# Keeping pre-computed weight sums in DRAM as two rounded halves

## The chip, the core and the metric

The kernel runs on one core of a Trainium2 chip. The metric is the device time of one execution in microseconds, as a median of runs. The engines are named as in the profile: PE multiplies matrices (PEld loads its stationary operand), DVE and ACT work on elements, POOL does small work, SP issues the DMAs.

## What is computed

A small decoder of two layers on 1024 tokens of width 1024, in float32. Layer 0 mixes tokens by a causal convolution module, layer 1 by sliding-window attention. Each layer then has a squared-ReLU MLP of width 4096 and a gated embedding, with layer norms between them. The part that matters here:

```python
def sq_relu_mlp(x, w_up, w_down):
    return jnp.square(jax.nn.relu(x @ w_up)) @ w_down
...
        x = layer_norm(DEEPNORM_ALPHA * x + sq_relu_mlp(x, mlp_w_up[i], mlp_w_down[i]),
                       mlp_ln_g[i], mlp_ln_b[i])
        x = x + (p[i] @ ple_w_proj[i]) * jax.nn.sigmoid(x @ ple_w_gate[i])
```

## The kernel before

**Arithmetic.** PE multiplies a rounded form of float32 (F32R). To keep precision each operand is split into a high half (the value rounded) and a low half (the value less its high half), and a product is three matmuls: high by high, high by low, low by high (`mm3`, line 676). Splitting costs one ACT cast and one DVE subtraction. On top of that the large products use a recursive scheme with seven block products in place of eight, which needs sums and differences of blocks of the weights: for the up weights S1 to S4 of a pair of units, for the down and gate weights t1 to t4.

**Weights ahead.** Some of that work is done well before it is needed. `low_half` (575) casts a half unit of 512 columns on ACT, subtracts on DVE in place and stores the low half in DRAM. `pair_ahead` (598) forms the four sums of a pair of up units, stores each sum in the DRAM tile `keep` (form in the trace) and its low half in another. `seven_ahead` (629) does the same for a quarter of the gate weights or half of the last chunk of the down weights: it forms t1 to t4, stores each sum (gate_t and down_t in the trace) and each low half (gate_low_t, down_low_t), and the low halves of three blocks that need no sum (gate_low_b, down_low_b). `pair_ahead` is called for one pair in layer 0 and two in layer 1, in the token-mixing stage (`PAIRS_AHEAD`, 74); `seven_ahead` in the up stage, at six points that `UP_WORK` (71) gives, with buffers from two quiet tiles (tag Q, which the trace shows as xh and xl).

**Weights used.** `prep` (549) brings a unit of 1024 columns into two buffers, wh and wl. Where a low half lies in DRAM it loads the sum into a third buffer, raw, casts raw to wh on ACT, and loads wl from DRAM. `Stream` (482) hands units out in the order of their use and refills a slot when the product that read it is done; there are 5 slots of wh and of wl, and 2 of raw (`SLOTS`, 48). In the last chunk of the down stage (`down_seven`, 1481, with `end`) a quarter t1 to t4 is loaded whole into a wl buffer by `quarter` (1476), and `form` (1450) casts it to the operand in two halves and loads the low half. The operands rotate over eight places in the xh and xl tiles, two for each product.

**The order of the work.** The program is first recorded and then ordered by a planner (`schedule`, 328). It goes through the recorded operations with a cost for each, assigns buffers first come, first served, and writes out one order for each engine; SP's DMA issues are among them. `later`, `after` and `slack` only shift priorities. Every instruction is issued from one place, so all have the same line, L479, in the trace; they are told apart by their tiles. Each engine executes its own list in order: an instruction that waits holds back what stands behind it.

**The gate stage** (`ple`, 1608) multiplies a 1024 by 1024 weight by seven block products in the order b11, b21, t4, t3, t2, t1, b22, two units each, four token tiles each.

Of the kernel before, what the change touches and what calls it, by code (L numbers as in the profile page):

```python
# [10 lines left out]
F32 = mybir.dt.float32  # L11
F32R = mybir.dt.float32r
AF = mybir.ActivationFunctionType
ALU = mybir.AluOpType

P = 128
T = 1024
# [3 lines left out]
HT = 512  # L21
# [490 lines left out]
class Emit:  # L512
# [33 lines left out]
        return self.nc.tile(tag, (P, HT), F32, "PSUM")  # L546


    def prep(self, ap, blocks=None, low=None):

        nc = self.nc
        raw = nc.tile("raw", (P, 1024), F32)
        wh = nc.tile("wh", (P, 1024), F32R)
        wl = nc.tile("wl", (P, 1024), F32R)
        if blocks:
            for j, kb in enumerate(blocks):
                cs = slice(j * 256, (j + 1) * 256)
                x = self.sb("X")
                for w, k in ((x, 0), (raw[:, cs], 1))[:: -1 if kb else 1]:
                    nc.sync.dma_start(w, ap[:, cs] if k else self.d["xT"][kb, :, 0:HT])  # L560
                self.split(raw[:, cs], wh[:, cs], wl[:, cs])
                self.split(x, *self.xs(kb, 0, HT))
            return wh, wl
        if low is not None:
            c = slice(0, low.n)
            nc.sync.dma_start(raw[:, c], ap)
            nc.scalar.copy(wh[:, c], raw[:, c])
            nc.sync.dma_start(wl.bitcast(F32)[:, c], low)
            return wh, wl
        nc.sync.dma_start(raw, ap)  # L570
        nc.scalar.copy(wh, raw)
        nc.vector.tensor_tensor(out=wl, in0=raw, in1=wh.bitcast(F32), op=ALU.subtract)
        return wh, wl

    def low_half(self, low, k, tag, raw):
# [4 lines left out]
        nc.vector.tensor_tensor(out=h, in0=raw, in1=h.bitcast(F32), op=ALU.subtract)  # L580
        nc.sync.dma_start(low[:, k * HT : (k + 1) * HT], h.bitcast(F32))

    def dram(self, name, n):
        self.nc.slots(name, [name])
        return self.nc.tile(name, (P, n), F32, "DRAM")
# [12 lines left out]
    def pair_ahead(self, i, f, tag):  # L598

        nc = self.nc  # L600
        w0, w1 = (self.d["w_up"][i, f + k] for k in range(2))
        keep = self.dram(f"form{i}_{f}", 4 * HT)
        low = [self.dram(f"form{i}_{f}_{k}", HT if k == 3 else 2 * HT) for k in range(4)]

        def form(k, out, x, y, op):
            nc.vector.tensor_tensor(out=out, in0=x, in1=y, op=op)
            nc.sync.dma_start(keep[:, k * HT : (k + 1) * HT], out)
            self.low_half(low[1 + k // 2], k % 2, tag, out)

        r1L, r1R, r0L = self.load(tag, w1, 0), self.load(tag, w1, 1), self.load(tag, w0, 0)  # L610
        self.low_half(low[3], 0, tag, r1R)
        form(1, r1R, r1L, r1R, ALU.add)
        form(2, r1L, r0L, r1L, ALU.subtract)
        self.low_half(low[0], 0, tag, r0L)
        form(0, r0L, r1R, r0L, ALU.subtract)
        r0R = self.load(tag, w0, 1)
        self.low_half(low[0], 1, tag, r0R)
        form(3, r0R, r0R, r0L, ALU.subtract)
        aps = w0, keep[:, 0 : 2 * HT], keep[:, 2 * HT : 4 * HT], w1[:, HT : 2 * HT]
        return [lambda ap=ap, l=l: self.prep(ap, low=l) for ap, l in zip(aps, low)]  # L620

    def seven_forms(self, name, n):

# [5 lines left out]
    def seven_ahead(self, name, quarters, k, tag):  # L629

        nc, g = self.nc, self.seven[name]
        b11, b21, b12, b22 = (self.load(tag, ap, c) for ap, c in quarters)

        def low(f, v):
            self.low_half(g[f][1], k, tag, v)

        def form(f, out, x, y):
            nc.vector.tensor_tensor(out=out, in0=x, in1=y, op=ALU.subtract)
            nc.sync.dma_start(g[f][0][:, k * HT : (k + 1) * HT], out)
            low(f, out)  # L640

        for f, v in (("b11", b11), ("b21", b21), ("b22", b22)):
            low(f, v)
        form("t1", b12, b12, b11)
        form("t2", b22, b22, b12)
        form("t3", b11, b22, b11)
        form("t4", b21, b21, b22)

    def work(self, what, k, tag):

# [11 lines left out]
    def gate_units(self, i, n):  # L662

        w, low = self.seven[f"gate{i}"][n]
        r = []
        for m in range(2):
            c = slice(m * 2 * HT, (m + 1) * 2 * HT)
            ap = w[:, c] if w else self.d["w_gate"][i, int(n[2]) - 1, 2 * int(n[1]) - 2 + m]
            r.append(lambda ap=ap, l=low[:, c]: self.prep(ap, low=l))
        return r  # L670

    def split(self, src, h, l):
# [777 lines left out]
    def form(self, src, tag=None, low=None):  # L1450

        hs = slice(0, HT), slice(HT, 2 * HT)
        if tag:
            f = [self.pair(tag, F32R) for k in range(2)]
        else:
            j = self.turn % KB
            self.turn += 1
            q = self.xT[((0, 0), (1, 0), (1, 1), (0, 1))[j // 2]]
            w = [x[:, j % 2 * 2 : j % 2 * 2 + 2, :].rearrange("p a b -> p (a b)") for x in q]
            f = [tuple(x[:, c] for x in w) for c in hs]  # L1460
        if low is not None:
            for k, c in enumerate(hs):
                self.nc.scalar.copy(f[k][0], src[k] if isinstance(src, list) else src[:, c])
                self.nc.sync.dma_start(f[k][1].bitcast(F32), low[:, c])
        elif isinstance(src, list) or tag:
            for k, c in enumerate(hs):
                self.split(src[k] if isinstance(src, list) else src[:, c], *f[k])
        else:
            self.split(src, *w)
        return f  # L1470
# [10 lines left out]
    def down_seven(self, i, cs, start, end, rest):  # L1481
# [6 lines left out]
        nc, d = self.nc, self.d  # L1488
# [3 lines left out]
        own = tags if end else (None, None)  # L1492
# [11 lines left out]
        def A(tag, what):  # L1504
            return load(tag, [self.hid[i][c, what] for c in cs])
# [4 lines left out]
        def halves(tag):  # L1510
            return [list(self.pair(spare)) if start else [self.sb(tag), self.sb(tag)] for c in cs]
# [9 lines left out]
            return out  # L1521

        def product(a, b, to, bank=None, own=(None, None), last=False, low=None, full=()):
            f = [[self.form(v, t, l) for v, t, l in zip(p, own, (None, low and made[low][1]))] for p in zip(a, b)]
            new = bank is None
            bank = [self.ps() for t in range(4)] if new else bank
            if last and to == [(0, 1)]:
                for k in range(3):
                    nc.move("ps", "tr")
            for t in range(4):  # L1530
                for k in range(n):
                    self.part(bank[t], *f[k], t, new and k == 0, k == n - 1, not new)
                for h, q in to:
                    self.add_to(t + 4 * h, q, bank[t], sums if (h, q) in full else None)
            for t in range(4 if last else 0):
                with nc.later(LATE if to == [(0, 1)] else 0):
                    self.layer_norm(t + 4 * to[0][0], gb, None, self.raw, sums[t + 4 * to[0][0]])
            mark = [o for o in nc.ops if o.eng == "tensor"][-1 - 24 * n]
            for k in range(2):
                if rest:  # L1540
                    t = rest.pop(0)
                    self.residual(i, t, tags[t % 2], mark)
            return bank
# [8 lines left out]
        if start:  # L1552
            c = cs[0]
# [5 lines left out]
        else:  # L1559
            a11, b11, a12, b21 = A("wh", (0, 0)), B("wl", 0, 0), None, None  # L1560
        if end:
            made = self.seven[f"down{i}"]
            sm = self.small(2 * NT)
            sums = [sm[:, 2 * t : 2 * t + 2] for t in range(NT)]

            def T(tag, f):
                return [self.quarter(tag, made[f][0])]

            one = product(a11, b11, [(0, 0)], low="b11")
            product(A("raw", (1, 0)), B("wl", 1, 0), [(0, 0)], low="b21", full=[(0, 0)])  # L1570
            product(A("wh", "s2"), T("wl", "t2"), [(1, 0)], one, low="t2")
            product(A("wh", "s1"), T("wl", "t1"), [(1, 1)], one, low="t1")
            s4, b22 = A("wh", "s4"), B("wl", 1, 1)

            self.raw = tuple(nc.tile(f"x{p}01", (P, 4, HT), F32) for p in "lh")
            gb = self.load_row("g", d["mlp_g"][i : i + 1]), self.load_row("g", d["mlp_b"][i : i + 1])
            product(s4, b22, [(0, 1)], one, (None, None), True, "b22", [(0, 1)])
            two = product(A("wh", "s3"), T("wl", "t3"), [(1, 1)], None, own, low="t3", full=[(1, 1)])
            product(A("raw", (1, 1)), T("wl", "t4"), [(1, 0)], two, own, True, "t4", [(1, 0)])
            return  # L1580
        one = product(a11, b11, [(0, 0)], own=("X", "X") if start else (None, None))
        product(a12 or A("raw", (1, 0)), b21 or B("wl", 1, 0), [(0, 0)])
# [511 lines left out]
```

## Time and profile before

| | |
|---|---|
| median of 3 runs | 2132.99 us (2129.67 to 2133.25) |
| profiled execution | 2129.71 us, span 2128.0 us |
| granted TensorE clock | 1.00 |
| busy share PE, PEld, DVE, ACT, POOL | 99%, 82%, 80%, 58%, 13% |
| DMA | 464.00 MB, mean 218 GB/s |

Names in the trace are written out<-in: `wh<-raw` is an instruction that reads raw and writes wh. ps and tr are PSUM banks. Idle time of an engine is given with the instruction that ended it. The stages of layer 0 are the convolution, the mixing of tokens, MLP up (about 445 to 645 us), MLP down (645 to 990), and the gate with the start of attention (990 to 1100); layer 1 has MLP up from 1440, MLP down from 1640 and the gate from 2010 to the end.

### The profile page before, as it was taken

How to read it: one execution, taken by the hardware profiler on the slowest of the kernel's cores; microseconds unless marked ns; L12 is line 12 of the kernel's file. 1: busy time of each engine (PE TensorE's matmuls, PEld its weight loads, DVE VectorE, ACT ScalarE, POOL GpSimd, SP SyncE). 2: the span in 40 equal slices, each digit the busy share in tenths (PEclk: the TensorE clock that was granted, in tenths of full speed). 3: DMA queues.
4: the chain of work that ended last, by engine and by line, in shares of the span. 5: the costliest groups of instructions: out<-in, count | busy, mean ns of one | idle time of the engine just before them, and what ended most of it. 6: DMA issues, size and time to landing. Idle time of an engine off the chain costs nothing.

```text
span 2128.0 us, 29691 instructions
## 1 busy us (share of the span) xinstructions
PE 2111.0 (99%) x9984; PEld 1748.6 (82%) x9984; DVE 1696.3 (80%) x2750; ACT 1239.3 (58%) x2309; POOL 280.1 (13%) x494
## 2 busy tenths in 40 slices
PE   9999999999999999999999999999999999999998
PEld 7888888878888888888787888888888888888877
DVE  8767698978776879876975888699887778888688
ACT  6655654766666533335756889457666663333484
POOL 0000024100000000001421666150000000000042
PEclk9999999999999999999999999999999999999999
DMA  7778954877778747565486022777877785565726
GB/s 255 230 217 281 284 203 155 293 249 268 264 244 258 271 162 227 193 193 183 164 306 224 22 79 83 220 239 255 284 270 261 265 304 176 178 229 171 258 88 219
DMA packets 219609, 464.00 MB, mean 218 GB/s; under 512 B 22080, under 2 KB 55488, under 8 KB 219456
## 3 DMA queue, kind: packets, MB, share of 16 engines
q1 hardware_dynamic: 219456, 462.11, 65.3%
q8 instruction: 78, 1.28, 0.3%
q14 instruction: 75, 0.61, 0.1%
HBM read 314.96 MB, written 147.06 MB: 217 GB/s over the span
## 4 chain that ended last, share of the span: by engine, by line
PE 86%; DVE 4%; ACT 4%; DMA 3%; issue 1%; POOL 1%; SPq 0%; ACTq 0%; POOLq 0%; DVEq 0%
PE ps L479 67%; PE tr L479 18%; ACT z L479 2%; DMA raw<-in_w_up_dram 1%; DVE wl L479 1%; DVE g L479 1%; POOL sm L479 1%; DVE t L479 1%; ACT wh L479 1%; ACT xh L479 1%; ACT t L479 1%; DVE B L479 0%; DMA raw<-in_w_kv_dram 0%; DMA down_low_t<-xl 0%; DVE X L479 0%
## 5 line engine op out<-in xcount | busy, mean ns | idle before, releaser
L479 PE MATMUL ps<-xh,xl 128*128 128x512 f32 x618 | 240.4, 389 | 0.0
L479 PE MATMUL ps<-xl,xh 128*128 128x512 f32 x618 | 240.4, 389 | 0.0
L479 PE MATMUL ps<-xh 128*128 128x512 f32 x618 | 240.4, 389 | 0.0
L479 POOL TENSOR_SCALAR sm<-sm 128x1 f32<-128x1 f32 x72 | 27.0, 379 | 1371.3 <-DVE E L479 610.7
L479 ACT CAST wh<-raw 128x1024 fp32r<-128x1024 f32 (+2 forms) x156 | 142.1, 915 | 105.6 <-PE ps L479 43.5
L479 PE MATMUL ps<-wh,xh 128*128 128x512 f32 (+1 forms) x460 | 182.9, 398 | 2.4 <-DVE t L479 1.5
L479 PE MATMUL ps<-xh,wh 128*128 128x512 f32 x472 | 183.9, 393 | 1.1 <-ACT bo L479 0.4
L479 PE MATMUL ps<-xl,wh 128*128 128x512 f32 x472 | 184.6, 392 | 0.0
L479 PE MATMUL ps<-xh,wl 128*128 128x512 f32 x472 | 184.1, 390 | 0.0
L479 PE MATMUL ps<-wl,xh 128*128 128x512 f32 (+1 forms) x460 | 183.3, 398 | 0.3 <-DMA wl<-gate_low_t 0.3
L479 PE MATMUL ps<-wh,xl 128*128 128x512 f32 (+1 forms) x460 | 182.7, 397 | 0.0
L479 DVE TENSOR_TENSOR wl<-raw,wh 128x1024 fp32r<-128x1024 f32 (+2 forms) x100 | 98.1, 983 | 59.8 <-ACT wh L479 59.4
L479 ACT CAST xh<-wh 128x1024 fp32r<-128x1024 f32 x76 | 79.7, 1049 | 111.8 <-PE ps L479 89.3
L479 ACT CAST wh<-g 128x512 fp32r<-128x512 f32 x136 | 80.9, 620 | 109.0 <-PE ps L479 66.7
L479 PEld LDWEIGHTS ps<-xh 128*128 128x128 f32 x618 | 116.0, 188 | 24.2
L479 PEld LDWEIGHTS ps<-xh,xl 128*128 128x128 f32 x618 | 116.1, 188 | 24.0
L479 PEld LDWEIGHTS ps<-xl,xh 128*128 128x128 f32 x618 | 116.0, 188 | 24.0
L479 DVE TENSOR_TENSOR wl<-g,wh 128x512 fp32r<-128x512 f32 x136 | 89.4, 685 | 35.3 <-ACT wh L479 35.2
L479 ACT ACTIVATE t<-t 128x512 f32<-128x512 f32 x144 | 91.0, 632 | 31.1 <-DVE t L479 29.2
L479 DVE TENSOR_TENSOR xl<-wh,xh 128x1024 fp32r<-128x1024 f32 x76 | 92.7, 1219 | 20.4 <-ACT xh L479 20.4
L479 PEld LDWEIGHTS ps<-xh,wh 128*128 128x128 f32 x472 | 88.8, 188 | 21.1 <-ACT bo L479 0.8
L479 PEld LDWEIGHTS ps<-xh,wl 128*128 128x128 f32 x472 | 88.8, 188 | 18.5
(425 smaller groups left out, 5623.5 us busy)
## 6 DMA issues: line engine op xcount, KB each, us to landing
wh<-hid SPq DMA_DIRECT2D x78, 512.0 KB, 4.2
raw<-in_w_up_dram SPq DMA_DIRECT2D x68, 512.0 KB, 4.2
wl<-in_w_down_dram SPq DMA_DIRECT2D x58, 512.0 KB, 4.8
hid<-zz SPq DMA_DIRECT2D x96, 256.0 KB, 4.7
z<-in_w_dw_dram SPq DMA_DIRECT2D x64, 288.0 KB, 4.3
hid<-t SPq DMA_DIRECT2D x64, 256.0 KB, 4.5
raw<-hid SPq DMA_DIRECT2D x30, 512.0 KB, 3.9
hid<-z SPq DMA_DIRECT2D x36, 256.0 KB, 4.7
```

The source lines that it names most:

```text
L479: getattr(getattr(nc, o.eng), o.name)(*a, **k)
```

## The change

The sums that are made ahead are stored in DRAM as their high half and their low half, and both are loaded as they are. The code that makes them now rounds the sum on ACT, stores the rounded half, subtracts in the place of the sum and stores the rest:

```diff
-    def prep(self, ap, blocks=None, low=None):
+    def prep(self, ap, blocks=None, low=None, halves=False):
 
         nc = self.nc
+        if halves:
+            wh = nc.tile("wh", (P, 1024), F32R)
+            wl = nc.tile("wl", (P, 1024), F32R)
+            for w, src in ((wh, ap), (wl, low)):
+                nc.sync.dma_start(w.bitcast(F32)[:, 0 : low.n], src)
+            return wh, wl
...
+    def high_half(self, high, k, tag, raw):
+
+        nc = self.nc
+        h = self.sb(tag, F32R)
+        nc.scalar.copy(h, raw)
+        nc.sync.dma_start(high[:, k * HT : (k + 1) * HT], h.bitcast(F32))
+        return h
+
+    def rest_half(self, low, k, raw, h):
+
+        nc = self.nc
+        r = raw.bitcast(F32R)
+        nc.vector.tensor_tensor(out=r, in0=raw, in1=h.bitcast(F32), op=ALU.subtract)
+        nc.sync.dma_start(low[:, k * HT : (k + 1) * HT], r.bitcast(F32))
...
-        def form(k, out, x, y, op):
+        def form(out, x, y, op):
             nc.vector.tensor_tensor(out=out, in0=x, in1=y, op=op)
-            nc.sync.dma_start(keep[:, k * HT : (k + 1) * HT], out)
-            self.low_half(low[1 + k // 2], k % 2, tag, out)
+
+        def halves(k, raw):
+            self.rest_half(low[1 + k // 2], k % 2, raw, self.high_half(keep, k, tag, raw))
...
         def form(f, out, x, y):
             nc.vector.tensor_tensor(out=out, in0=x, in1=y, op=ALU.subtract)
-            nc.sync.dma_start(g[f][0][:, k * HT : (k + 1) * HT], out)
-            low(f, out)
+            return f, out, self.high_half(g[f][0], k, tag, out)
...
-        form("t1", b12, b12, b11)
-        form("t2", b22, b22, b12)
-        form("t3", b11, b22, b11)
-        form("t4", b21, b21, b22)
+        t1 = form("t1", b12, b12, b11)
+        t2 = form("t2", b22, b22, b12)
+        rest(*t1)
+        rest(*form("t3", b11, b22, b11))
+        rest(*form("t4", b21, b21, b22))
+        rest(*t2)
...
-        if low is not None:
+        if src is None:
+            for x, ap in enumerate(low):
+                for k, c in enumerate(hs):
+                    self.nc.sync.dma_start(f[k][x].bitcast(F32), ap[:, c])
+        elif low is not None:
...
-            product(A("wh", "s2"), T("wl", "t2"), [(1, 0)], one, low="t2")
+            product(A("wh", "s2"), [None], [(1, 0)], one, low="t2")
```

In `pair_ahead` the order of the steps changes so that a sum is only overwritten after its last use, and `gate_units` and `down_seven` ask for halves where the unit is a sum (t1 to t4). Units without a sum are loaded and cast as before.

More of the change, by code (lines that the diff above doesn't have):

```diff
@@ L603, in pair_ahead @@
         low = [self.dram(f"form{i}_{f}_{k}", HT if k == 3 else 2 * HT) for k in range(4)]
-        def form(k, out, x, y, op):
+        def form(out, x, y, op):
             nc.vector.tensor_tensor(out=out, in0=x, in1=y, op=op)
-            nc.sync.dma_start(keep[:, k * HT : (k + 1) * HT], out)
-            self.low_half(low[1 + k // 2], k % 2, tag, out)
+        def halves(k, raw):
+            self.rest_half(low[1 + k // 2], k % 2, raw, self.high_half(keep, k, tag, raw))
         r1L, r1R, r0L = self.load(tag, w1, 0), self.load(tag, w1, 1), self.load(tag, w0, 0)
         self.low_half(low[3], 0, tag, r1R)
-        form(1, r1R, r1L, r1R, ALU.add)
-        form(2, r1L, r0L, r1L, ALU.subtract)
+        form(r1R, r1L, r1R, ALU.add)
+        form(r1L, r0L, r1L, ALU.subtract)
+        halves(2, r1L)
         self.low_half(low[0], 0, tag, r0L)
-        form(0, r0L, r1R, r0L, ALU.subtract)
+        form(r0L, r1R, r0L, ALU.subtract)
+        halves(1, r1R)
         r0R = self.load(tag, w0, 1)
         self.low_half(low[0], 1, tag, r0R)
-        form(3, r0R, r0R, r0L, ALU.subtract)
+        form(r0R, r0R, r0L, ALU.subtract)
+        halves(0, r0L)
+        halves(3, r0R)
         aps = w0, keep[:, 0 : 2 * HT], keep[:, 2 * HT : 4 * HT], w1[:, HT : 2 * HT]
-        return [lambda ap=ap, l=l: self.prep(ap, low=l) for ap, l in zip(aps, low)]
+        return [lambda ap=ap, l=l, h=j in (1, 2): self.prep(ap, low=l, halves=h) for j, (ap, l) in enumerate(zip(aps, low))]
     def seven_forms(self, name, n):
@@ L638, in form, with rest @@
             nc.vector.tensor_tensor(out=out, in0=x, in1=y, op=ALU.subtract)
-            nc.sync.dma_start(g[f][0][:, k * HT : (k + 1) * HT], out)
-            low(f, out)
+            return f, out, self.high_half(g[f][0], k, tag, out)
+        def rest(f, v, h):
+            self.rest_half(g[f][1], k, v, h)
         for f, v in (("b11", b11), ("b21", b21), ("b22", b22)):
             low(f, v)
-        form("t1", b12, b12, b11)
-        form("t2", b22, b22, b12)
-        form("t3", b11, b22, b11)
-        form("t4", b21, b21, b22)
+        t1 = form("t1", b12, b12, b11)
[4 more added lines that the diff above has]
+        rest(*t2)
     def work(self, what, k, tag):
@@ L668, in gate_units @@
             ap = w[:, c] if w else self.d["w_gate"][i, int(n[2]) - 1, 2 * int(n[1]) - 2 + m]
-            r.append(lambda ap=ap, l=low[:, c]: self.prep(ap, low=l))
+            r.append(lambda ap=ap, l=low[:, c]: self.prep(ap, low=l, halves=w is not None))
         return r
@@ L1523, in product @@
         def product(a, b, to, bank=None, own=(None, None), last=False, low=None, full=()):
-            f = [[self.form(v, t, l) for v, t, l in zip(p, own, (None, low and made[low][1]))] for p in zip(a, b)]
+            f = [[self.form(v, t, l) for v, t, l in zip(p, own, (None, low and (made[low] if p[1] is None else made[low][1])))] for p in zip(a, b)]
             new = bank is None
@@ L1564, in down_seven @@
             sums = [sm[:, 2 * t : 2 * t + 2] for t in range(NT)]
-            def T(tag, f):
-                return [self.quarter(tag, made[f][0])]
             one = product(a11, b11, [(0, 0)], low="b11")
             product(A("raw", (1, 0)), B("wl", 1, 0), [(0, 0)], low="b21", full=[(0, 0)])
-            product(A("wh", "s2"), T("wl", "t2"), [(1, 0)], one, low="t2")
-            product(A("wh", "s1"), T("wl", "t1"), [(1, 1)], one, low="t1")
+            product(A("wh", "s2"), [None], [(1, 0)], one, low="t2")
+            product(A("wh", "s1"), [None], [(1, 1)], one, low="t1")
             s4, b22 = A("wh", "s4"), B("wl", 1, 1)
@@ L1577, in down_seven @@
             product(s4, b22, [(0, 1)], one, (None, None), True, "b22", [(0, 1)])
-            two = product(A("wh", "s3"), T("wl", "t3"), [(1, 1)], None, own, low="t3", full=[(1, 1)])
-            product(A("raw", (1, 1)), T("wl", "t4"), [(1, 0)], two, own, True, "t4", [(1, 0)])
+            two = product(A("wh", "s3"), [None], [(1, 1)], None, own, low="t3", full=[(1, 1)])
+            product(A("raw", (1, 1)), [None], [(1, 0)], two, own, True, "t4", [(1, 0)])
             return
```

## The prediction

> **What bounds the kernel now.** I read the page first: the span and the busy time of each engine.
>
> ```profile
> span 2128.0 us, 29691 instructions
> PE 2111.0 (99%) x9984; PEld 1748.6 (82%) x9984; DVE 1696.3 (80%) x2750; ACT 1239.3 (58%) x2309; POOL 280.1 (13%) x494
> ```
>
> PE, the matmul engine, is idle for 17.0 us of the span (2128.0 - 2111.0). Nothing in the change alters a matmul, so it can only act on those 17 us or add to them. ACT, which it relieves, is busy 58% of the time and is not the bound. The second view is the busy time by stretch, cut at the stages: MLP up (445 to 645), MLP down (645 to 990), the end of layer 0 with its gate (990 to 1100), then the same three of layer 1. The columns are the stretch, its length, then busy time and count of PE, PEld, DVE, ACT, POOL, then clock, DMA share and GB/s.
>
> ```profile
> 445.00:645.00 200.00, 199.41 (x877) 163.87 (x876) 154.95 (x243) 126.39 (x217) 0.00 (x0) 1.00 0.79 264
> 645.00:990.00 345.00, 344.88 (x1522) 285.22 (x1521) 267.04 (x345) 154.07 (x208) 0.00 (x0) 1.00 0.67 223
> 990.00:1070.00 80.00, 78.09 (x372) 63.70 (x372) 71.56 (x125) 59.54 (x108) 33.77 (x39) 1.00 0.35 119
> 1070.00:1100.00 30.00, 28.87 (x148) 23.55 (x147) 25.44 (x34) 20.03 (x34) 7.63 (x6) 1.00 0.92 317
> 1440.00:1640.00 200.00, 199.73 (x879) 164.30 (x878) 166.97 (x264) 133.43 (x228) 0.00 (x0) 1.00 0.81 269
> 1640.00:2010.00 370.00, 370.00 (x1634) 306.43 (x1633) 288.52 (x380) 174.09 (x244) 0.00 (x0) 1.00 0.68 228
> 2010.00:2062.00 52.00, 51.26 (x253) 42.30 (x253) 41.99 (x72) 38.32 (x75) 23.18 (x38) 1.00 0.12 42
> 2062.00:2128.00 66.00, 59.64 (x275) 48.60 (x273) 53.43 (x83) 32.25 (x52) 14.64 (x5) 0.99 0.70 239
> ```
>
> Length minus PE busy is PE's idle time: 0.6 and 0.3 us in the two up stretches, 0.1 and 0.0 in the down stretches, 3.0 from 990 to 1100, 0.7 and 6.4 from 2010 on, most of the 6.4 behind the last matmul. So of the three places where the change works, down offers nothing and the gates offer what there is. The third view, PE's waits, names who ended them (total, times, longest; ps and tr are PSUM banks, released by whoever read them last); the two that a DMA ended are shown where they count.
>
> ```profile
> PE ps L479 <- ACT t L479: 1.1, 3, 0.5
> PE ps L479 <- ACT zz L479: 0.9, 1, 0.9
> PE tr L479 <- ACT zz L479: 0.6, 1, 0.6
> PE ps L479 <- ACT bo L479: 0.4, 1, 0.4
> ```
>
> **Part one: loads and casts.** Three groups of loads change, here with their count, size and median time to landing, and behind them the casts that they feed.
>
> ```profile
> raw<-gate_t SPq DMA_DIRECT2D x16, 512.0 KB, 5.8
> wl<-down_t SPq DMA_DIRECT2D x8, 512.0 KB, 5.1
> raw<-form SPq DMA_DIRECT2D x6, 512.0 KB, 6.1
> L479 ACT CAST wh<-raw 128x1024 fp32r<-128x1024 f32 x111 | 115.9, 1050 | 83.4 <-PE ps L479 31.4 <-DMA raw<-in_w_gate_dram 17.4 <-PE tr L479 16.4
> L479 ACT CAST xh<-wl x6: 611/616/624, 1996.4 to 2004.0; 128x512 fp32r<-128x512 f32 x6
> ```
>
> The 16 gate loads and 6 form loads go straight into wh instead of raw, and their casts go: 22 x 1.050 = 23.1 us of ACT. The 8 down loads become 16 of 256 KB, straight into the operand; 16 half casts go: 16 x 0.616 = 9.9 us. ACT loses 33 us in all. Bytes stay as they were; SP issues 8 more DMAs. Most of the 33 us lies beside PE's work, so by itself it is worth nothing; what counts is where a cast stood ahead of something that PE waited for. The timeline of the second gate shows two such places.
>
> ```profile
> 2070.10 1.05 ACT L479 CAST wh<-raw 128x1024 fp32r<-128x1024 f32 x1 [4.19 <-DMA raw<-gate_t]
> 2071.57 0.58 ACT L479 COPY zz<-tr 128x512 f32<-128x512 f32 x1
> 2072.20 0.50 PE L479 MATMUL tr<-wh,xh 128*128 128x512 f32 x1 [0.61 <-ACT zz L479]
> 2074.56 1.04 ACT L479 CAST wh<-raw 128x1024 fp32r<-128x1024 f32 x1
> 2075.50 0.58 ACT L479 COPY zz<-ps 128x512 f32<-128x512 f32 x1
> 2076.13 0.50 PE L479 MATMUL ps<-wh,xh 128*128 128x512 f32 x1 [0.92 <-ACT zz L479]
> ```
>
> ACT runs in order. It stood 4.19 us before a cast whose data was still on its way, and the copy that empties a PSUM bank stood behind it. Without the cast the first copy runs as much as 4 us sooner and PE's 0.61 us goes; the second copy runs 1.04 us sooner, more than the 0.92 us that PE waited. **Gain: 0.61 + 0.92 = 1.53 us.** The ACT waits for t and bo, up to 0.5 and 0.4 us each, are not tied to a cast that goes: I count nothing there, with 0.9 us as the end of a gain.
>
> Against it stands what becomes late next. Until now the high half was fetched early into one of the 2 raw buffers, and only the low half waited for PE to release a weight slot; now both halves wait for it. SP and PE in the second gate, PE in the first, and two pieces of the chain of work that ended last (start, length to landing):
>
> ```profile
> 2010.97 1.61 SPq L479 DMA_DIRECT2D raw<-gate_t  x2
> 2060.90 1.70 SPq L479 DMA_DIRECT2D wl<-gate_low_t  x2
> 2065.96 0.40 PE L479 MATMUL tr<-wh,xh 128*128 128x512 f32 x1
> 2096.63 0.32 SPq L479 DMA_DIRECT2D wl<-gate_low_t  x1
> 2100.55 0.50 PE L479 MATMUL tr<-wl,xh 128*128 128x512 f32 x1 [0.55 <-DMA wl<-gate_low_t]
> 1070.68 0.50 PE L479 MATMUL ps<-wl,xh 128*128 128x512 f32 x1 [0.29 <-DMA wl<-gate_low_t]
> 2063.53 6.55 DMA raw<-gate_t
> 2096.63 3.88 DMA wl<-gate_low_t
> ```
>
> The high halves of 2010.97 came some 50 us ahead of the low halves of 2060.90. At 2096.63 a slot came free, its low half took 3.88 us to land and PE stood 0.55 us for it; the first gate has the same at 1070.68 with 0.29 us. There PE's wait now grows by what the second half adds. Bounds: nothing, if the 16 DMA engines (0.70 busy in that stretch) take both at once; 2.67 us, if the pair lands as late as the 6.55 us of the load in the crowd at 2063.53. I take 512 KB at the 317 GB/s of the busiest stretch: 524,288 B / 317 GB/s = 1.65 us, since both are issued back to back into the same queue. **Loss: 2 x 1.65 = 3.30 us** (ends 0 and 5.34).
>
> The Trainium skill, DMA: Bandwidth & Descriptors, section Specifications, gives about 358 GB/s of HBM bandwidth per core; by it the second half would add an estimated 1.46 us and the loss would be 2.9 us; no run so far shows that rate.
>
> The other units of a gate have slack. The tightest is that of 2060.90: its first use is six matmuls behind 2065.96, at 0.227 us each (345.0 us / 1522 in the down stretch) 2067.3; by 3.88 + 1.65 it lands at 2066.4, 0.9 us ahead. That cover is thin, and is where the slower rival begins. In down the loads are covered by the PE that never pauses between 1640 and 2010: an operand's buffers come free three products before they are needed again (form takes 2 of 8 for each product), 48 matmuls or 10.9 us each, against 5.1 us of landing. I cost the 8 extra issues at nothing; the upper end is their own time, 8 x 0.32 = 2.6 us of SP, if nothing hid them.
>
> **Part two: making the halves.** The sum used to be stored behind the DVE instruction that made it; now ACT rounds it first, the rounded half is stored, DVE subtracts in place and the rest is stored. Casts, subtractions and stores stay the same in number.
>
> ```profile
> L479 ACT CAST xl<-xh 128x512 fp32r<-128x512 f32 x84 | 49.2, 613 | 5.3 <-DVE xh L479 4.4 <-DMA gate_low_b<-xl 0.9
> L479 DVE TENSOR_TENSOR xl<-xh,xl 128x512 fp32r<-128x512 f32 x84 | 54.3, 683 | 0.0
> L479 SPq DMA_DIRECT2D gate_t<-xh x32: 319/508/1122, 433.6 to 1602.0; - x32
> ```
>
> The high store goes out 0.61 us later (one cast), and a source buffer is held 0.68 us longer (one subtraction). The last gate store of layer 1 is at 1602.0 and the gate loads come some 400 us behind (2010.97 above); I cost this at nothing. The forms of the up stage have less room: their last store is at 1429.4, their last load at 1442.6.
>
> ```profile
> L479 SPq DMA_DIRECT2D form<-t x22: 319/322/802, 1361.0 to 1429.4; - x22
> L479 SPq DMA_DIRECT2D raw<-form x6: 320/381/446, 397.5 to 1442.6; - x6
> ```
>
> Thirteen microseconds cover one cast and one subtraction, 1.3 us. Without that cover the 1.3 us would stand once in each layer.
>
> **The sum.** Against the profiled execution (2129.71 us, 1.7 over its span): -1.53 + 3.30 = +1.77, so 2131.5. That execution lies 3.28 us under the median of 2132.99; carried over, the prediction is 2132.99 + 1.77 = **2134.8 us**. The open ends move it from -1.53 - 0.9 = -2.4 us to -1.53 + 5.34 + 2.6 + 2.6 = +9.0 us, which is 2130.6 to 2142.0.
>
> **The rivals.** A measurement of this kernel can tell about 0.2%, 4.3 us, from no change.
>
> *Both halves late everywhere (slower).* Place: the starts of the gate products that use sums, four of them in each of two gates. Price: 1.65 us each, 8 x 1.65 = 13.2, less the 1.53 gained: +11.7, 2144.7. It decides from the point where a released slot is needed less than 3.88 + 1.65 = 5.5 us later; two starts are there already, and two more lift the sum to +5.1, past the bound. For it: the slack of 0.9 us above, and one in-order queue in which the waiting load holds back the residual and output DMAs behind it.
>
> ```profile
> SPq L479 <- PE ps L479: 166.3, 69, 34.0
> ```
>
> SP already stands 166 us for PE. The Trainium skill, same page, section Anatomy of one DMA, says a semaphore wait is done by the issuing sequencer before dispatch, so what is queued behind it waits too; this row agrees. Against it: five slots, of which a product uses two for 10.9 us, leave most loads about twice the time they need. Chance 0.34.
>
> *Freed ACT and raw buffers help PE everywhere (faster).* The order of all engines is planned anew, and the two raw buffers lose 22 users, so that untouched weights come sooner too. Its ceiling is PE's waits in the up and gate stages: 0.6 + 0.3 + 3.0 + 0.7 and, in the last stretch, 0.61 + 0.92 + 0.55: 6.7 us, 2126.3. To be told from no change it must remove two thirds of them, the DMA ones included, which it makes later. Chance 0.18.
>
> *The gain is hidden and the loss too.* ACT falls by 33 us and the time by nothing: 2133.0. It lies in the same bin as the forecast; together 0.48, of which my forecast's side has 0.28.
>
> The time is in the range 2127 to 2145 8 times in 10: the ends of the open costs, most of the slower rival and all but the ceiling of the faster one. The chances are 0.18 faster, 0.48 the same, 0.34 slower.
>
> **What would show it.** Right: ACT's busy time near 1206, loads of gate_t into wh, no PE wait for ACT zz at the second gate, and PE waits for DMA of gate_t or gate_low_t of 1 to 3 us in each gate, PE's idle time elsewhere unchanged. Wrong: DMA waits of PE at four or more product starts, or in the down stages; a PE idle total under 13 us; or PE waits that move to transposes because the planner wove them differently, which I can't price from this trace.

## The result, and the profile after

| | before | changed |
|---|---|---|
| median of 19 runs each | 2133.01 us | 2129.62 us |
| ratio to before, 95% interval | | 0.9987 (0.9981 to 0.9993) |
| profiled execution, span | 2128.0 us | 2126.4 us |

By the ratio the changed kernel is 2.8 us faster (0.13% of 2133; the interval is 1.5 to 4.1 us); the medians differ by 3.4 us. One of the 19 runs of before took 3009 us and is not in the ratio. The forecast was 1.8 us slower, so the sign was wrong.

The page of the changed kernel: span, busy time of the engines, and its DMA issues with count, size and median time to landing:

```profile
span 2126.4 us, 29679 instructions
PE 2108.6 (99%) x9984; PEld 1748.0 (82%) x9984; DVE 1696.1 (80%) x2745; ACT 1210.1 (57%) x2271; POOL 290.5 (14%) x499
wh<-gate_t SPq DMA_DIRECT2D x16, 512.0 KB, 6.8
wh<-form SPq DMA_DIRECT2D x6, 512.0 KB, 5.8
```

Its casts from raw, among the groups of instructions by form, and PE's waits for gate_t, with one wait that the kernel before did not have (total, times, longest):

```profile
L479 ACT CAST wh<-raw 128x1024 fp32r<-128x1024 f32 x89 | 93.2, 1053 | 61.9 <-PE ps L479 31.6 <-PE tr L479 14.7 <-DMA raw<-in_w_gate_dram 8.4
```

```profile
PE tr L479 <- DMA wh<-gate_t: 1.4, 1, 1.4
PE ps L479 <- DMA wh<-gate_t: 1.0, 1, 1.0
PE ps L479 <- DVE zz L479: 1.2, 1, 1.2
```

The edit did what it says: 22 casts of whole units are gone (111 before, 89 now), ACT has 38 instructions less (2309 to 2271; 22 and 16 half casts), and the loads go into wh. PE waits for DMA once in each gate, 1.4 and 1.0 us, where it waited 0.55 and 0.29 us for the low half alone. In the second gate the copies out of PSUM run with no cast from raw ahead of them (ACT's timeline):

```profile
2068.86 0.58 ACT L479 COPY zz<-tr 128x512 f32<-128x512 f32 x1
2071.85 0.58 ACT L479 COPY zz<-ps 128x512 f32<-128x512 f32 x1
```

From 2062 to 2090 PE is now busy for all of the 28 us, where it was for 26.47. The columns are as in the prediction; the changed kernel and then the one before:

```profile
2062.00:2090.00 28.00, 28.00 (x129) 23.23 (x128) 27.96 (x46) 14.02 (x25) 9.34 (x2) 1.00 0.77 288
```

```profile
2062.00:2090.00 28.00, 26.47 (x120) 21.28 (x119) 25.76 (x41) 18.04 (x29) 6.03 (x2) 1.00 0.82 290
```

A place that the forecast had set to nothing changed too: the start of the first up stage. The same columns for 425 to 500, the kernel before and then the changed one:

```profile
425.00:500.00 75.00, 73.89 (x323) 59.98 (x322) 58.32 (x94) 46.90 (x82) 0.00 (x0) 1.00 0.77 255
```

```profile
425.00:500.00 75.00, 75.00 (x332) 61.88 (x331) 61.52 (x99) 47.77 (x83) 0.00 (x0) 1.00 0.81 266
```

PE's idle time there falls from 1.11 us to nothing. The timelines of SP, DVE and PE show what stands in front of it: in the kernel before, DVE begins a pair's sums when a raw buffer is loaded, ACT casts them behind it, the copy that empties a PSUM bank comes after the casts, and PE stands 0.52 us ahead of 441.22.

```profile
431.90 0.37 SPq L479 DMA_DIRECT2D raw<-in_w_up_dram  x1
438.13 0.69 DVE L479 TENSOR_TENSOR g<-raw 128x512 f32<-128x512 f32 x1 [2.21 <-DMA raw<-in_w_up_dram]
441.22 0.72 PE L479 MATMUL ps<-A,wh 128*128 128x512 f32 x2 [0.52 <-ACT t L479]
```

In the changed kernel the load at the same place in the order is issued 0.40 us earlier and DVE starts 1.58 us earlier; the rest of the 1.58 us is a shorter time from issue to DVE's start (5.05 us, where it was 6.23):

```profile
431.50 0.33 SPq L479 DMA_DIRECT2D raw<-in_w_up_dram  x1
436.55 0.69 DVE L479 TENSOR_TENSOR g<-raw 128x512 f32<-128x512 f32 x1 [3.89 <-DMA raw<-in_w_up_dram]
```

So four things moved: the gate's ACT waits went, its DMA waits grew, the up stage's start waits less, and PE has a new wait of 1.2 us for DVE zz, at 1148.53 in the attention of layer 1. PE's idle time as a whole did not fall: it is 17.8 us of the changed span (2126.4 - 2108.6), where it was 17.0. What fell in this pair of profiles is PE's busy time, by 2.4 us for the same 9984 matmuls. (A second profile of the changed kernel, below as change_again, has 16.5 us idle and 2.7 us less busy than before.) But the planner also wrote another order for every engine, and 2.8 us could be that alone. The experiments take these apart. Every ratio is to the kernel before on the same chip, with its 95% interval; half a permille is about 1 us.

### The profile page after: what moved, and what is told of

Read it like the earlier page. It is cut to its first block, busy times and chain, and to the rows that moved or that the text cites. A ratio compares the mean times of both kernels' runs of the same rounds, so it can differ in the third digit from the quotient of the medians.

```text
span 2126.4 us, 29679 instructions
## 1 busy us (share of the span) xinstructions
PE 2108.6 (99%) x9984; PEld 1748.0 (82%) x9984; DVE 1696.1 (80%) x2745; ACT 1210.1 (57%) x2271; POOL 290.5 (14%) x499
## 4 chain that ended last, share of the span: by engine, by line
PE 87%; DVE 5%; DMA 3%; ACT 3%; issue 1%; POOL 1%; SPq 0%; DVEq 0%; ACTq 0%; POOLq 0%
PE ps L479 68%; PE tr L479 19%; ACT z L479 1%; DVE t L479 1%; POOL sm L479 1%; DVE g L479 1%; DMA wh<-gate_t 1%; DMA X<-in_xT_dram 0%; DVE wl L479 0%; DMA t<-proj 0%; DMA hid<-zz 0%; DMA z<-in_w_dw_dram 0%; DVE z L479 0%; DVE B L479 0%; DMA raw<-in_w_up_dram 0%
## 5 line engine op out<-in xcount | busy, mean ns | idle before, releaser
L479 ACT CAST wh<-raw 128x1024 fp32r<-128x1024 f32 (+2 forms) x134 | 119.3, 894 | 81.2 <-PE ps L479 46.6
```

Source lines behind the costliest of these rows:

```text
L479: getattr(getattr(nc, o.eng), o.name)(*a, **k)
```

## The experiments

**One part at a time.** First the three places where halves are loaded, one by one.

`gate_only`: the gate's producer and loads from the change; the pairs and the last chunk of down keep the old code (`seven_ahead_sum` is the old `seven_ahead`). Against before:

```diff
-            r.append(lambda ap=ap, l=low[:, c]: self.prep(ap, low=l))
+            r.append(lambda ap=ap, l=low[:, c]: self.prep(ap, low=l, halves=w is not None))
...
-                self.seven_ahead(what, [(w[j, q], k) for q in range(2) for j in range(2)], k, tag)
+                self.seven_ahead_sum(what, [(w[j, q], k) for q in range(2) for j in range(2)], k, tag)
```

> Only the 16 gate loads take rounded halves; the pairs of the up stage and the last chunk of down stay as before. Theory A (casts in ACT's order): the changed kernel is 2.8 us faster than before, about half of it because the two PE waits for ACT zz in the second gate (0.61 and 0.92 us) go; this kernel loses them too, PE's DMA waits in each gate are 0.7 to 1.5 us, and the whole is 1 to 2 us faster than before. Theory B (another order): what counts is that the planner wrote another order, wherever the edit is; then the second gate's waits need not go, and the time can lie anywhere within 3 us of before.

0.9998 (0.9989 to 1.0006). The waits for ACT zz are gone and the DMA waits are 1.0 and 0.9 us, as theory A has it, yet there is no gain. At 425 to 500 PE waits as much as before or more (ACT t 1.1, bo 0.4 us).

`pair_only`: from the change only `pair_ahead` and the new branch of `prep`. Against before:

```diff
-        return [lambda ap=ap, l=l: self.prep(ap, low=l) for ap, l in zip(aps, low)]
+        return [lambda ap=ap, l=l, h=j in (1, 2): self.prep(ap, low=l, halves=h) for j, (ap, l) in enumerate(zip(aps, low))]
```

> Only the 6 loads of pair sums at the start of the up stages take rounded halves. Theory A: the PE waits for ACT zz in the second gate stay, 1.5 us in all; the waits at the start of the first up stage (0.5 and 0.4 us) go if they came from the raw buffers, and the time is 0 to 1.5 us under before. Theory B: the second gate changes too although its code does not, and the time can lie anywhere within 3 us of before.

0.9991 (0.9982 to 1.0000). The smallest part, 6 loads, has the lowest ratio of the three, but its interval reaches no change, and `producer_only` below, which alters no load, has 0.9992. The gate keeps a wait for ACT zz (0.8 us); 425 to 500 has no idle PE time at all:

```profile
425.00:500.00 75.00, 75.00 (x332) 61.88 (x331) 60.67 (x98) 46.54 (x81) 0.00 (x0) 1.00 0.81 264
```

`down_only`: the new `form`, and the new producer for down alone. Against before:

```diff
-            product(A("wh", "s2"), T("wl", "t2"), [(1, 0)], one, low="t2")
+            product(A("wh", "s2"), [None], [(1, 0)], one, low="t2")
```

> Only the 8 loads of t1 to t4 of the last chunk of down take rounded halves. Theory A: PE never pauses there, so nothing, within 1 us of before; the waits for ACT zz in the second gate stay. Theory B: any time within 3 us of before, by the other order.

0.9995 (0.9986 to 1.0004): nothing that can be told. ACT zz stays, 1.3 and 0.9 us.

`producer_only`: the sums are rounded, stored and subtracted in the new way, but loaded through raw and cast.

Against the changed kernel, in the gate as an example:

```diff
-            r.append(lambda ap=ap, l=low[:, c]: self.prep(ap, low=l, halves=w is not None))
+            r.append(lambda ap=ap, l=low[:, c]: self.prep(ap, low=l))
```

> The sums are rounded, stored and subtracted as in the change, but loaded into raw and cast again (the cast of a rounded value leaves it as it is), so ACT keeps its 33 us. Theory A: no gain, 0 to 1 us over before, since the gate's ACT waits stay and the high store comes one cast later; a cost of 1 us or more in the up stages (PE waiting for ACT t or DVE bo) would explain why gate_only, with the same gate, gained only 0.4 us. Theory B: any time within 3 us of before.

0.9992 (0.9984 to 1.0001). The producer costs nothing that can be told; ACT zz stays. From 425 to 500 PE idles 0.52 us, half of what it did, though every pair sum still passes through raw, so a gain of this size in order 1 can be had without any change of the loads:

```profile
425.00:500.00 75.00, 74.48 (x327) 60.95 (x327) 59.94 (x97) 46.55 (x81) 0.00 (x0) 1.00 0.77 256
```

```profile
PE tr L479 <- ACT zz L479: 1.5, 1, 1.5
PE ps L479 <- ACT zz L479: 0.9, 1, 0.9
```

`gate_down`: the change with the old `pair_ahead`. Against the changed kernel:

```diff
-        def halves(k, raw):
-            self.rest_half(low[1 + k // 2], k % 2, raw, self.high_half(keep, k, tag, raw))
...
+            nc.sync.dma_start(keep[:, k * HT : (k + 1) * HT], out)
+            self.low_half(low[1 + k // 2], k % 2, tag, out)
```

> The change without its pairs: gate and down take rounded halves, the pairs of the up stage as before. If the waits at the start of the first up stage go because the pair sums no longer pass through raw, they stay here (1 us or more of PE waits for ACT t and bo at 440 to 446), and the time is 1 to 2 us over the changed kernel, 0.9985 to 0.9997 of before. If they go by the order, they can go here too.

1.0008 (0.9999 to 1.0016), against 0.9987 with the pairs. The wait at the start of the up stage is back (stretch), and the second gate's DMA wait was 2.2 us in this execution (waits). Half a microsecond behind that wait the granted clock, the third column from the right, was 0.50 for 3.4 us:

```profile
425.00:500.00 75.00, 74.05 (x325) 60.65 (x324) 60.04 (x97) 47.49 (x82) 0.00 (x0) 1.00 0.77 258
```

```profile
PE tr L479 <- DMA wh<-gate_t: 2.2, 1, 2.2
```

```profile
2103.60:2107.00 3.40, 3.40 (x9) 2.67 (x9) 0.69 (x1) 0.59 (x1) 0.00 (x0) 0.50 0.69 265
```

At the 0.227 us of a matmul in the prediction, 15 would have started there in place of 9, so the stretch lost an estimated 1.4 us on top of the wait. 32 of the 38 casts are gone here, and there is no gain; but as this late load costs more than in the changed kernel, the distance to 0.9987 need not be the pairs alone.

**The order alone.** A constant of the planner changes the order on every engine and what is computed not at all (a few additions that may run on DVE or POOL change sides). `order_only` and `change_other_order` (order 2) have `lat = 201.0` for 200.0; `before_order3` and `change_order3` have 0.4428 for 0.4427 in a matmul's cost; `before_order4` and `change_order4` have `lat = 199.0`.

```diff
-        lat = 200.0
+        lat = 201.0
...
-            return max(109.0, f * 0.4427 + 5.5 * (f < HT))
+            return max(109.0, f * 0.4428 + 5.5 * (f < HT))
```

> The kernel before, with one constant of the planner changed (the time after which a freed buffer may be used again, 201 in place of 200): the same instructions, in another order on each engine. Theory A: the order alone moves the time by less than 1 us, and the gate keeps PE waits for ACT behind a cast of gate_t. Theory B: the time moves by 2 to 5 us one way or the other, as much as the change moved it.

> The changed kernel with the planner's constant for a freed buffer at 201 in place of 200, the counterpart of order_only (which lay 0.04% over before, interval -0.05 to +0.13%). Theory A (the change itself gives the gain, by the casts that no longer stand in ACT's order): 2 to 3 us under order_only, so 1 to 3 us under before, and no PE wait for ACT zz in the second gate. Theory B (the gain is that of one lucky order): the gain of 2.8 us shrinks to within 1 us of order_only or turns round.

> The kernel before, with the planner's cost of a matmul column at 0.4428 ns in place of 0.4427: the same instructions in a third order. Spread theory (order alone moves the time by about 0.1%): anywhere within 3 us of before; the second gate keeps PE waits for ACT zz of 1 to 2.5 us in all.

> The changed kernel with the same constant at 0.4428. If the change has a gain of its own, it lies 1 to 3 us under before_order3, as it lies 2.8 us under before in the first order; if the first order was lucky, the difference to before_order3 is under 1 us or has the other sign. In either case the second gate has no PE wait for ACT zz, and a PE wait for DMA wh<-gate_t of 0.7 to 1.5 us in each gate.

> The kernel before with the constant for a freed buffer at 199: a fourth order. Spread theory: within 0.3% of before, either side.

> The changed kernel with that constant at 199. If the change has a gain of its own of 2 to 3 us on top of the scatter by order (the three pairs so far: -2.8, -0.4 and -6.4 us), it lies 1 to 5 us under before_order4; a time over it by more than 1 us would speak for order alone.

> The changed kernel once more, unaltered, on the chip of this call: 0.9981 to 0.9993 of before as measured, and a second profile of one program, whose PE idle time by stage tells how much a single execution scatters: I expect stages to agree within 1 us.

| order | before | changed | difference | PE idle 425 to 500, before / changed |
|---|---|---|---|---|
| 1 | 1 | 0.9987 (0.9981 to 0.9993); again 0.9982 (0.9973 to 0.9991) | -0.13, -0.18% | 1.11 / 0.00 us |
| 2 | 1.0004 (0.9995 to 1.0013) | 1.0002 (0.9994 to 1.0011) | -0.02% | 0.31 / 1.19 us |
| 3 | 1.0027 (1.0017 to 1.0038) | 0.9997 (0.9988 to 1.0006) | -0.30% | 2.39 / 0.00 us |
| 4 | 0.9996 (0.9988 to 1.0005) | 0.9983 (0.9974 to 0.9991) | -0.13% | 1.90 / 0.00 us |

(The last column is the stretch less PE's busy time. A difference of two ratios is known to some 0.12 points, from the two intervals; order 1 is known better.) Order alone moves the kernel before by -0.04 to +0.27%, as much as the change does, so one comparison could not have told them apart. But the changed kernel is never the slower one, and in three of four orders it is faster by more than 0.1%. With four orders a gain of the change itself is likely, not shown. Where the gain is smallest, in order 2, the start of the up stage is also where it did not help; where it is largest, in order 3, it removed most there (before_order3, then change_order3):

```profile
425.00:500.00 75.00, 72.61 (x318) 58.94 (x317) 58.61 (x95) 47.02 (x82) 0.00 (x0) 1.00 0.76 246
```

```profile
425.00:500.00 75.00, 75.00 (x332) 61.88 (x331) 61.29 (x99) 47.23 (x83) 0.00 (x0) 1.00 0.81 266
```

That stretch is not all of order 3, though. The profile of before_order3 also has a PE wait of 2.0 us early in the down stage of layer 1, where change_order3 has no PE idle time, and behind it again 3.4 us at half the clock (wait, then stretch):

```profile
PE tr L479 <- ACT t L479: 2.0, 1, 2.0
1711.70:1715.00 3.30, 3.30 (x9) 2.52 (x9) 0.94 (x2) 0.00 (x0) 0.00 (x0) 0.50 0.69 169
```

pair_only and pair_only_order3 have a wait like it in layer 0 (2.0 and 2.1 us), so such waits come and go with the order. Such a stretch takes the mean clock of an execution to 0.999 (half of 3.4 us in 2138), so the three of seven executions of before_order3 at 1.000 are without it. Their median is 2135.55 us; that of the nine of change_order3 at 1.000 is 2132.43 us. So 3.1 us are left of the 4.4 us between the medians of all.

My expectation for before_order3 was wrong on the gate: it has no wait for ACT zz at all. That wait is a matter of where the planner puts the cast, not of the cast being there. The two profiles of the changed kernel in order 1 differ in span by 1.6 us (2126.4 and 2124.8), and the DMA waits were 1.4 and 1.0 in one and 1.8 and 1.4 us in the other; one execution says no more than that. From 990 to 1070 PE idles 1.67 us in one and 2.82 us in the other, more apart than the 1 us that I had expected.

**Raw buffers or casts.** `pair_only_order3` is `pair_only` in order 3.

> Only the pairs, in the third order (matmul column 0.4428), to be held against before_order3 (1.0027 of before, PE waits for ACT t 1.9 and ACT bo 0.4 us at the start of the up stage). If raw is the cause: those 2.3 us go and the time is 2 to 3 us under before_order3. If order is: waits of any size there.

1.0003 (0.9994 to 1.0011), 0.24% under before_order3, with no idle PE time from 425 to 500. The pairs alone give most of what the change gives in that order too (0.30%), but the kernel that both are held against is the one with the extra wait in down. Pairs differ from before in two ways: 6 casts are gone, and 6 sums no longer pass through raw. `pair_sums_in_zz` and its twin in order 3 keep the sums, the casts and the low halves as before and only load the pair sums into another buffer:

```diff
-        raw = nc.tile("raw", (P, 1024), F32)
+        raw = nc.tile(home, (P, 1024), F32)
...
+        homes = "raw", "zz", "zz", "raw"
+        return [lambda ap=ap, l=l, h=h: self.prep(ap, low=l, home=h) for ap, l, h in zip(aps, low, homes)]
```

> The kernel before, with one line of it changed: the 6 pair sums of the up stages are loaded into the single zz buffer (free then) in place of one of the 2 raw buffers, and cast from there on ACT as before. If freed raw buffers are the cause at the start of the first up stage, its PE waits for ACT t and bo (1.1 us) go, though all casts are still there, and the time is 0 to 2.5 us under before, as with pair_only (0.9991). If the missing casts are the cause, the waits stay and there is no gain.

> The same in the third order, against before_order3 (1.0027; 2.3 us of those waits). Raw as the cause: the 2.3 us go and the time is near pair_only_order3 (1.0003). Casts as the cause: the waits stay, the time near 1.0027.

0.9989 (0.9981 to 0.9998), and 0.9996 (0.9987 to 1.0005) against 1.0027. With every cast in place a gain as large as that of the pairs is there in both orders, so it does not need the casts to go. The stretch in order 1 and in order 3:

```profile
425.00:500.00 75.00, 74.47 (x327) 60.91 (x327) 62.43 (x100) 48.72 (x84) 0.00 (x0) 1.00 0.79 275
```

```profile
425.00:500.00 75.00, 74.88 (x330) 61.55 (x329) 62.60 (x101) 49.26 (x85) 0.00 (x0) 1.00 0.80 272
```

Of the 1.11 us half goes (0.53 stay), of the 2.39 us all but 0.12. So taking the pair sums out of raw goes with a shorter wait here, casts or no casts. In order 1, though, producer_only has the same 0.52 us with the sums still in raw, so half of the wait can go without a freed buffer.

**What the load stood behind.** The traces show what held the load. In the kernel before, the buffer of the load at 431.90 had been free for 0.9 us: DVE's last read of it ended at 430.98. SP was late, because a load of the buffer t from DRAM, 431.00, and a store behind it stood ahead in its list, and the load of t had waited 3.6 us for a store to its place (hid) to land. In the changed kernel DVE's read ends later, at 431.47, but SP waits for that read alone, and the load of t comes behind. DVE, SP and SP's wait ahead of the load, before and then changed:

```profile
430.29 0.69 DVE L479 TENSOR_TENSOR wl<-raw,wh 128x512 fp32r<-128x512 f32 x1
431.00 0.32 SPq L479 DMA_DIRECT2D t<-hid  x1
SPq L479 <- DMA hid<-t: 3.6, 1, 3.6
```

```profile
430.78 0.69 DVE L479 TENSOR_TENSOR wl<-raw,wh 128x512 fp32r<-128x512 f32 x1
437.47 0.32 SPq L479 DMA_DIRECT2D t<-hid  x1
SPq L479 <- DVE wl L479: 1.7, 1, 1.7
```

The 20 profiles of this study divide by that place. In ten the load of t stands ahead and waits 3.5 to 4.0 us for hid; there PE idles 0.52 to 2.39 us from 425 to 500. In the other ten SP waits for DVE's read of raw; there PE idles 0 to 0.53 us, in seven of them nothing. In orders 1, 3 and 4 all nine profiles with the pair sums out of raw are of the second kind and all eight with the sums in raw of the first; in order 2 it is the reverse (order_only of the second kind, change_other_order and t1_from_raw_order2 of the first). So what the freed raw buffers change is where the planner puts this load, and that turns with the order. No run moves this one load and nothing else.

**The gate's terms.** `cast_on_pool` takes the gate's 16 casts off ACT and leaves the early load of the high half. Against before:

```diff
-            nc.scalar.copy(wh[:, c], raw[:, c])
+            (nc.gpsimd.tensor_copy if pool else nc.scalar.copy)(wh[:, c], raw[:, c])
```

> The kernel before, with the 16 casts of gate_t from raw to wh done on POOL in place of ACT: ACT loses these 17 us, nothing else of the change is in it, and the high half still comes early into raw. Theory A: PE's waits for ACT zz in the second gate go as in the changed kernel, its DMA wait stays at 0.3 to 0.6 us in each gate because only the low half is late, and the time is 1.5 to 2.5 us under before. Rival C (it is the raw buffers or the loads that help, not the casts): no gain, 0 to 1 us. A slow POOL (over 2 us for each cast) could cost PE waits of its own.

1.0053 (1.0040 to 1.0065), slower, so it tells little of the rival. The waits for ACT zz are gone; a larger wait in each gate took their place, and the casts on POOL (shortest, median and longest in ns) took up to 3.6 us:

```profile
L479 POOL CAST wh<-raw x16: 1038/1146/3637, 980.2 to 2101.7; 128x1024 fp32r<-128x1024 f32 x16
```

```profile
PE ps L479 <- DVE zz L479: 6.1, 1, 6.1
PE tr L479 <- DVE zz L479: 4.9, 1, 4.9
```

`t1_from_raw` and `t1_from_raw_order2` are the change with t1, whose load PE waits for, put back to raw and cast.

```diff
-            r.append(lambda ap=ap, l=low[:, c]: self.prep(ap, low=l, halves=w is not None))
+            r.append(lambda ap=ap, l=low[:, c]: self.prep(ap, low=l, halves=w is not None and n != "t1"))
```

> The changed kernel, but the two units of t1 of each gate load their high half into raw and cast it, as before the change; the other sums stay as in the change. Theory A with a late second half: PE's wait for DMA wh<-gate_t (1.4 us in the second gate, 1.0 in the first) falls back to 0.3 to 0.6 us for the low half, 1 to 1.6 us are gained on the changed kernel, 3.5 to 4.5 us on before. Rival D (the DMA wait only takes the place of another wait, since PE is given other work ahead of it): no gain on the changed kernel, within 0.7 us of it.

> t1_from_raw with the constant for a freed buffer at 201, to be held against change_other_order (1.0002 of before). If the late second half of t1 costs what its DMA waits show, it lies 1 to 2 us under change_other_order and has DMA waits of PE under 0.6 us in each gate; if the 2.3 us by which t1_from_raw beat the change was order alone, the difference has either sign.

0.9976 (0.9967 to 0.9986) in order 1, the fastest kernel of this study, and 1.0009 (1.0000 to 1.0018) in order 2, where the change has 1.0002. The DMA waits of the two gates fell from 2.4 to 0.6 us in order 1, from 2.2 to 1.4 us in order 2. The wait of 1.2 us for DVE zz between 1100 and 1330 is gone in both; the seven profiles that load t1 as halves all have it, the 13 others do not. A gain that is not there in order 2 is not shown to be one of t1: the 0.9976 stands as a measured time, not as a better idea.

## Why the prediction was wrong, point by point

**PE is the bound, down offers nothing.** Right in that the 33 us of ACT appear as 29 us less busy time and are worth nothing by themselves, and that down_only changes nothing that can be told. Not borne out is that the change can only act on the 17 us of PE's idle time: in the profiles these became 17.8 and 16.5 us, and the shorter spans came mostly with less busy time, 2.4 and 2.7 us. Why the same matmuls are busy for less is not known.

**Gain in the gate, 1.53 us.** Right in order 1: both waits went, and none is left in any of the five profiles of the changed kernel. But it is a term of the order: before has 1.5, 1.5, 0 and 2.2 us of it in the four orders.

**Loss in the gate, 3.30 us.** The mechanism was right; the size was not, and one term was missing. The two DMA waits grew from 0.84 to 2.42 us, by 1.6 us (2.4 us in the second profile). SP's issues, the piece of the chain and PE in the changed kernel:

```profile
2094.08 0.32 SPq L479 DMA_DIRECT2D wl<-gate_low_t  x1
2094.49 0.38 SPq L479 DMA_DIRECT2D wh<-gate_t  x1
```

```profile
2094.49 5.84 DMA wh<-gate_t
```

```profile
2100.47 0.47 PE L479 MATMUL tr<-wh,xh 128*128 128x512 f32 x1 [1.44 <-DMA wh<-gate_t]
```

From the slot's release at 2094.08 to the last half is 2094.49 + 5.84 - 2094.08 = 6.25 us, 2.37 us more than the 3.88 before and near my upper bound of 2.67. By the rate of the Trainium skill (DMA: Bandwidth & Descriptors, Specifications) it would have been an estimated 1.46 us; the trace does not agree with its 2.37 us, and other DMAs stood in the queue too. PE waits only 0.9 us longer, for the planner put other matmuls in between: from the slot's release to the wait PE had 4.95 us of work, where it had 3.37. I had left PE's order as it was. The missing term is the wait of 1.2 us for DVE zz that comes with t1 as halves. The gate's terms together, -1.53 + 1.6 + 1.2, are a loss of about 1.3 us, and gate_only and gate_down measure about zero or a small loss.

**The step that failed** is the sentence on the ACT waits for t and bo at the start of the up stage: "not tied to a cast that goes: I count nothing there". They were not tied to a cast, but they were open to the change: DVE's sums wait for a load into raw, ACT's casts for DVE, PSUM's copy for ACT, PE for that, and the load itself for what stands ahead of it in SP's list. I stopped at the last link, ACT. In order 1 that is 1.1 us of PE's time, which went to nothing. The second step is the loss, put at 3.30 us and measured at 1.6. With these two the sum is -1.53 + 1.6 - 1.1 = -1.0 us and has the measured sign; but with the new wait it is +0.2 us, and PE's idle time as a whole moved by +0.8 us in one profile of the changed kernel and by -0.5 in the other. So the waits name the steps that were wrong and do not add up to the gain: the spans of the two profiles differ by 1.6 us, the ratio says 2.8 (1.5 to 4.1), and where these come from stays open.

**The rivals.** Both halves late at every start (2144.7 us) did not come: PE waits for gate_t once in each gate, not at four starts. The faster rival had named both things that show at the start of the up stage, the new order and the raw buffers that lose 22 users (6 of them matter there). Its ceiling counted most of PE's waits in the up and gate stages, the DMA ones included, and those grew. The hidden gain is what down came to.

**What stays open**: how the 2.8 us come about when PE's idle time hardly moves, whether four orders stand for all, and why the planner places the load of the up stage as it does in each order.

## What to carry to other kernels

Follow a wait back past the engine that ended it, through the buffers to the queue: here a load three links away was late for what stood ahead of it in SP's list, and not for its buffer. Where a planner writes the order, compare the change with the kernel before in several orders; here order alone moved the time by up to 0.27%, more than the change. A load that comes late costs PE less than its lateness where other matmuls can be put ahead of it (0.9 of 2.37 us here). Check that the waits you name add up to the change in idle time before you call them the gain.

## What the runs showed of the hardware

A cast of 128x1024 took 1.05 us on ACT; on POOL it took 1.15 us at the median and up to 3.64 us beside the other work. Two loads of 512 KB issued 0.41 us apart on the one queue landed 6.25 us after the first issue, where the low half without the high one took 3.88 us; other DMAs were in the queue both times.

Of the PE pauses inside the 20 profiles, three of 2.00, 2.04 and 2.21 us (before_order3, pair_only, gate_down) were followed by 3.4 us at a granted clock of 0.50, and the two of 4.9 and 6.1 us in cast_on_pool by 6.8 us. One of 2.13 us (pair_only_order3) was not, nor was any of 1.9 us or less. So a wait of some 2 us could cost an estimated 1.2 to 1.4 us beyond itself, from the 9 matmuls of each such stretch above.
